# A two-layer decoder trunk on one core: weight sums, a late accumulation and turns put elsewhere in the MLP

## The chip, the cores and the metric

The kernel runs on one core of a Trainium2 chip. A core has TensorE (PE in the profile), VectorE (DVE), ScalarE (ACT), GpSimd (POOL) and SyncE (SP, which here only issues DMAs); GpSimd issues DMAs too, among them those that add to what lies at their destination. The metric is the device time of one execution in microseconds. The kernel before took 1130.81 us, the median of 3 runs (1129.59 to 1131.3).

## What is computed

512 tokens of width 1024 go through two layers. Layer 0 mixes tokens by gated linear attention, layer 1 by stick-breaking attention over shared keys and values. Behind each mixer stand a layer norm, an MLP and another layer norm:

```python
h = layer_norm(DEEPNORM_ALPHA * h + mix, ln_g[layer, 0], ln_b[layer, 0])
h = layer_norm(DEEPNORM_ALPHA * h + sq_relu_mlp(h, mlp_w_up[layer], mlp_w_down[layer]),
               ln_g[layer, 1], ln_b[layer, 1])
...
def sq_relu_mlp(x, w_up, w_down):
    h = jax.nn.relu(x @ w_up)
    return (h * h) @ w_down
```

The MLP's inner width is 4096, all in fp32. The change is in the MLP alone.

## The kernel before

**Products.** A product of fp32 matrices is made from three matmuls: each operand is split into a rounded part `hi` (made by ScalarE: L70 for weights, L98 for activations) and a remainder `lo` (VectorE: L72, L99), and hi·hi, hi·lo and lo·hi are summed. The two MLPs take most of the time: layer 0's from about 207 to 541 us of the span, layer 1's from about 783 to 1111. Between them lie keys, values and attention; the attention's output projection (L1292) ends where layer 1's MLP begins.

**Chunks and steps.** Each MLP runs in four chunks of 1024 of the inner width. A chunk has an `up` product and a `down` product, and each is a 2×2 block product made with seven block products instead of eight, the seven steps of `steps`. So each step needs a sum of activation blocks and a sum of weight blocks. The operands of up are the turned (transposed) tiles T, with the sums in place: step 2 takes `sum3` (L830), step 3 `sum4` (L725 into tmp), step 4 `sum5` (L725 into T), step 5 `sum6` (L842). Those of down are the squared activations s. Matmuls of up are at L899 (48 in a step), of down at L948 (24). After a step VectorE adds the product from PSUM: L915 in up, L167 or L169 in down.

**Weights.** Class `Blocks` holds a product's weights in tiles B of 512 KB, each block in two halves. Block (0,0) and (1,0) are plain; (0,1) and (1,1) are loaded by SP (L741) and then get (0,0) or (0,1) added by an accumulating DMA from GpSimd (L743). Step 3 takes (0,0)+(1,1), which `onto` makes in place just ahead of its splits, and step 6 (1,0)+(0,0). If the block is listed in `by`, the sum is a DMA on GpSimd's queue (L765), otherwise an addition on VectorE (L767). In the last chunk's down of each layer both sums are listed, elsewhere only (1,0) or none. Step 4's weights are a fresh load (`plain`, tiles raw, L64). There are eight B tiles, so the loads for the next product wait until the splits of the current one have read its tiles.

**Start of an MLP.** The four token tiles get their norm one after the other: VectorE makes statistics (L177, L182), GpSimd `ve` and `rs` (L183, L184), VectorE centres the tile (L190), TensorE turns it (L267), ScalarE copies the turned tile (L270). Tiles 2 and 3 are late: their turns are called from within steps 0 and 1 of the first up. The loads of (0,0) and (1,0) of that up are issued by GpSimd (L876) behind a small copy `pin` (L932) which waits for tile 3's `rs`.

**Order.** The program names the order by its writing, and a scheduler of the framework orders each engine's instructions by when it expects them to be ready; instructions passed through `keep` stay in the order in which they are written. Each engine then runs its list strictly in that order. `run_all` makes blocks two steps and operands up to two steps ahead; `between` runs between a step's matmuls and its read.

Of the kernel before, what the change touches and what calls it, by code (L numbers as in the profile page):

```python
# [34 lines left out]
def yoco_kernel(ctx: ExitStack, tc: tile.TileContext, x, gla_w_in, gla_w_a2, gla_b_a, gla_norm_g,  # L35
# [693 lines left out]
    class Blocks:  # L729


        def __init__(self, pool, weights, order, by):
            self.pool, self.w, self.by, self.b = pool, weights, by, {}
            self.load(order)

        def load(self, order, start=lambda **to: nc.sync.dma_start(**to)):
            for k, j, other in order:
                got = []
                for h in range(2):
                    b = self.pool.tile([P, 1024], F32, tag="B", bufs=8, name=nm("B"))  # L740
                    start(out=b.rearrange("p (a b) -> p a b", a=2), in_=self.w(k, h, j))  # L741
                    if other:
                        nc.gpsimd.dma_start(out=b.rearrange("p (a b) -> p a b", a=2), in_=self.w(other[0], h, other[1]),  # L743
                                            accum_op=ALU.add)
                    got.append(b)
                self.b[k, j] = got

# [14 lines left out]
        def onto(self, a, b, h):  # L762
            x, y = self.b[a][h], self.b[b][h]
            if a in self.by:
                keep(nc.gpsimd.dma_start(out=x, in_=y, accum_op=ALU.add))  # L765
            else:
                keep(tt(x, x, y, op=ALU.add))  # L767
            hi, lo = split_tile(x, 2, keep)
            return [(hi[:, i, :], lo[:, i, :]) for i in range(2)]
# [14 lines left out]
    def mlp(l, hT, late, vec, done, ready=None):  # L784
# [26 lines left out]
        def steps(a11, a12, a21, a22, weights, part, read, order, by=(), plain=None, ops=None, after=None):  # L811

            made, t = [], []

# [17 lines left out]

            def sum4():
                minus(t[0], t[0], a11())
                return operand(t[0])

            def sum5(apart=False):
                minus(a12(), a12(), t[0])
                return operand(a12(), apart)

            def sum6(apart=False):
                tt(a11(), a11(), a21(), op=ALU.subtract)  # L842
                return operand(a11(), apart)

            makes = [lambda: operand(a11()), lambda: operand(a12()), sum3, sum4, sum5, sum6, lambda: operand(a22())]
            if ops is not None:
                if not ops:
                    ops.update({0: views([hT.a[0]]), 1: views([hT.a[1]])})
                    kinds = {2: sum3, 3: sum4, 4: lambda: sum5(True), 5: lambda: sum6(True), 6: makes[6]}
                    new = lambda i: (lambda: ops[i]) if i < 2 else (lambda: ops.setdefault(i, kinds[i]()))  # L850
                else:
                    new = lambda i: lambda: ops[i]
                makes = [new(i) for i in range(7)]
# [11 lines left out]
            def step(n):  # L865
# [9 lines left out]
                if after and n == 0:  # L875
                    me.rest = lambda: (after(), made[0].load(AHEAD[:2], lambda **to: keep(nc.gpsimd.dma_start(**to))))  # L876
# [7 lines left out]
        def up(c, also=()):  # L884
# [5 lines left out]
            def part(a, b, banks, opens, closes, n):  # L890
# [3 lines left out]
                for m, (k, f) in enumerate(at):  # L894
                    if c == 0 and late and (n == 0 and m == 13 and len(late) > 1 or n == 1 and m == 4):
                        late.pop(0)()
# [29 lines left out]
            else:  # L926
                plain = [ready[:4], ready[4:]] if ready else [pieces_512(mlp_w_up[l], 512 * k, 4, 0) for k in range(2)]
                last = hs[3].rs

# [4 lines left out]
                made = steps(r[0], r[2], r[1], r[3], w, part, read, AHEAD[2:], ((1, 0),), plain, ops, after)  # L934
# [32 lines left out]
        for c in range(NC):  # L967
# [3 lines left out]
            todo += down(c, q, (range(NT) if l == 0 else (2, 3)) if ends else (), ((0, 0), (1, 0)) if ends else ((1, 0),),  # L971
                         turns[2:] if c == 0 else ())

        def run_all():
            for n, step in enumerate(todo):
# [8 lines left out]
                def between():  # L984
                    if n == 0:
                        step.rest()
                    if n == 1:
                        todo[2].make_operand()
                    if 0 < n <= 5:
# [523 lines left out]
```

## Time and profile before

| what | us |
|---|---|
| median of 3 runs | 1130.81 |
| the profiled execution, its own time | 1129.37 |
| its span, first to last instruction | 1127.6 |
| mean granted TensorE clock | 0.989 of full |

The profile is of one execution, whose own time is 1.77 us above its span and 1.44 us below the median. In a row of a timeline the first number is the start in us of the span, the second the length, then engine, line, operation, tiles and shapes; xN says that N like instructions stand together, and the bracket is the idle time of that engine ahead of the row and what ended it. A row of the table by windows gives, for a stretch, its length, the busy time and count of TensorE, its weight loads, VectorE, ScalarE and GpSimd, the granted clock, the share of time that the DMA engines were busy, and GB/s.

The last rows of the table of groups that bear on the change are these: the two kinds of split, in which VectorE and ScalarE spend the most time.

```profile
L72 DVE TENSOR_TENSOR lo<-B,hi 128x1024 fp32r<-128x1024 f32 x206 | 247.5, 1221 | 84.2 <-ACT hi L70 82.0
L70 ACT ACTIVATE hi<-B 128x1024 fp32r<-128x1024 f32 x206 | 213.5, 1054 | 158.5 <-DVE B L767 65.6
```

### The profile page before, as it was taken

How to read it: one execution, taken by the hardware profiler on the slowest of the kernel's cores; microseconds unless marked ns; L12 is line 12 of the kernel's file. 1: busy time of each engine (PE TensorE's matmuls, PEld its weight loads, DVE VectorE, ACT ScalarE, POOL GpSimd, SP SyncE). 2: the span in 40 equal slices, each digit the busy share in tenths (PEclk: the TensorE clock that was granted, in tenths of full speed). 3: DMA queues.
4: the chain of work that ended last, by engine and by line, in shares of the span. 5: the costliest groups of instructions: out<-in, count | busy, mean ns of one | idle time of the engine just before them, and what ended most of it. 6: DMA issues, size and time to landing. Idle time of an engine off the chain costs nothing. (4 is left out here: it accounts for less than half of the span.)

```text
span 1127.6 us, 16741 instructions
## 1 busy us (share of the span) xinstructions
PE 1091.5 (97%) x6463; PEld 942.9 (84%) x6463; DVE 898.9 (80%) x1083; ACT 669.8 (59%) x963; POOL 182.8 (16%) x217
## 2 busy tenths in 40 slices
PE   9999999989999999999999999997899999999987
PEld 7888888888798898997788787786897988989965
DVE  4488639898988879868898887696989888788667
ACT  4455437676466475564765667765865674655634
POOL 1021210402111111111303001212121011011112
PEclk9999999999999999999999999998999999999989
DMA  7262394779959869687757325456798599597673
GB/s 218 74 182 67 129 256 134 185 215 229 221 155 245 206 154 257 150 222 165 205 126 197 95 87 119 117 135 142 222 245 218 145 222 247 139 244 188 193 180 75
DMA packets 121443, 197.53 MB, mean 175 GB/s; under 512 B 14042, under 2 KB 39002, under 8 KB 121364
## 3 DMA queue, kind: packets, MB, share of 16 engines
q1 hardware_dynamic: 90580, 127.78, 35.4%
q0 software_dynamic: 28320, 63.97, 30.7%
q10 hardware_dynamic: 2464, 4.72, 1.2%
q8 instruction: 51, 0.84, 0.3%
q14 instruction: 28, 0.23, 0.1%
HBM read 176.52 MB, written 3.15 MB: 159 GB/s over the span
## 5 line engine op out<-in xcount | busy, mean ns | idle before, releaser
L72 DVE TENSOR_TENSOR lo<-B,hi 128x1024 fp32r<-128x1024 f32 x206 | 247.5, 1221 | 84.2 <-ACT hi L70 82.0
L70 ACT ACTIVATE hi<-B 128x1024 fp32r<-128x1024 f32 x206 | 213.5, 1054 | 158.5 <-DVE B L767 65.6
L948 PE MATMUL ps<-hi,T 128*128 128x512 f32 x896 | 286.4, 397 | 11.5 <-ACT T L98 8.1
L899 PE MATMUL ps<-T,hi 128*128 128x256 f32 x1280 | 233.0, 284 | 4.4 <-DVE T L99 2.0
L948 PEld LDWEIGHTS ps<-hi,T 128*128 128x128 f32 x896 | 170.7, 191 | 52.6 <-ACT T L98 10.2
L899 PEld LDWEIGHTS ps<-T,hi 128*128 128x128 f32 x1280 | 199.5, 192 | 8.2 <-ACT T L98 2.7
L899 PE MATMUL ps<-T,lo 128*128 128x256 f32 x640 | 179.7, 284 | 3.7 <-DVE lo L72 3.7
L948 PE MATMUL ps<-lo,T 128*128 128x512 f32 x448 | 177.6, 396 | 0.0
L899 PEld LDWEIGHTS ps<-T,lo 128*128 128x128 f32 x640 | 121.9, 192 | 5.0 <-DVE lo L72 4.8
L70 ACT ACTIVATE hi<-raw 128x1024 fp32r<-128x1024 f32 x88 | 91.1, 1057 | 43.5 <-PE ps L94 9.3
L72 DVE TENSOR_TENSOR lo<-raw,hi 128x1024 fp32r<-128x1024 f32 x86 | 103.0, 1217 | 16.5 <-ACT hi L70 16.1
L948 PEld LDWEIGHTS ps<-lo,T 128*128 128x128 f32 x448 | 85.7, 191 | 17.8 <-DVE lo L72 0.7
L899 PE MATMUL ps<-A,hi 128*128 128x256 f32 x512 | 92.5, 283 | 0.0
L98 ACT ACTIVATE T<-s 128x1024 fp32r<-128x1024 f32 (+1 forms) x52 | 51.5, 993 | 53.2 <-DVE s L842 37.0
L93 PE MATMUL ps<-T,hi 128*128 128x512 f32 (+1 forms) x200 | 79.7, 399 | 0.4 <-DVE k L99 0.4
L899 PEld LDWEIGHTS ps<-A,hi 128*128 128x128 f32 x512 | 79.9, 192 | 0.0
L95 PE MATMUL ps<-T,lo 128*128 128x512 f32 (+1 forms) x200 | 76.5, 382 | 0.0
L94 PE MATMUL ps<-T,hi 128*128 128x512 f32 (+1 forms) x200 | 76.4, 382 | 0.0
L743 POOL DMA_DIRECT2D B<-in_mlp_w_down_dram x32 | 38.5, 1202 | 232.0 <-DVE lo L72 103.1
L169 DVE TENSOR_TENSOR h<-h,ps 128x512 f32<-128x512 f32 x108 | 71.4, 680 | 4.2 <-PE ps L948 3.5
L899 PE MATMUL ps<-A,lo 128*128 128x256 f32 x256 | 72.4, 283 | 0.0
L743 POOL DMA_DIRECT2D B<-in_mlp_w_up_dram x32 | 38.8, 1221 | 159.6 <-DMA B<-in_mlp_w_up_dram 45.0
(234 smaller groups left out, 1903.9 us busy)
## 6 DMA issues: line engine op xcount, KB each, us to landing
B<-in_mlp_w_down_dram SPq DMA_DIRECT2D x64, 512.0 KB, 5.3
B<-in_mlp_w_up_dram SPq DMA_DIRECT2D x56, 512.0 KB, 4.8
B<-in_mlp_w_up_dram POOLq DMA_DIRECT2D x40, 512.0 KB, 8.7
B<-in_mlp_w_down_dram POOLq DMA_DIRECT2D x32, 512.0 KB, 9.5
B<-B POOLq DMA_DIRECT2D x28, 512.0 KB, 5.5
raw<-in_mlp_w_up_dram SPq DMA_DIRECT2D x24, 512.0 KB, 5.6
raw<-in_gla_w_in_dram SPq DMA_DIRECT2D x20, 512.0 KB, 3.8
raw<-in_mlp_w_down_dram SPq DMA_DIRECT2D x16, 512.0 KB, 9.8
```

Of the source, the lines that this page charges most:

```text
L70: keep(nc.scalar.activation(hi, raw, AF.Copy))
L72: keep((on or nc.vector).tensor_tensor(lo, raw, hi.bitcast(F32), op=ALU.subtract))
L93: keep(nc.tensor.matmul(ps, lhsT=a[0], rhs=b[0], start=first, stop=False))
L94: keep(nc.tensor.matmul(ps, lhsT=a[0], rhs=b[1], start=False, stop=False))
L95: keep(nc.tensor.matmul(ps, lhsT=a[1], rhs=b[0], start=False, stop=last))
L98: keep(nc.scalar.activation(hi, ps, AF.Copy))
L169: nc.vector.tensor_tensor(h, h, ps, op=op)
L743: nc.gpsimd.dma_start(out=b.rearrange("p (a b) -> p a b", a=2), in_=self.w(other[0], h, other[1]), accum_op=ALU.add)
L899: nc.tensor.matmul(to, lhsT=b[k][x][:, fs], rhs=a(k)[:, y], start=opens and f % 2 == 0 and (k, x, y) == (0, 0, LO), stop=closes and (k, x) ...
L948: nc.tensor.matmul(banks[s], lhsT=a(k)[:, x][:, P * s:P * s + P], rhs=b[k][y], start=opens and (k, x, y) == (0, LO, 0), stop=closes and (k ...
```

## The change

It has four parts.

1. In the last chunk's down of both layers the first weight sum, (0,0)+(1,1), is made by VectorE and no longer by DMAs.
2. In the first up of both layers, `sum4` and the first half of step 3's weight sum are made right behind step 2's operand, ahead of `sum5`; the second half follows later, between the operands. `sum5` and `sum6` there now keep the written order.
3. In layer 1 the accumulation into (1,1) of the first up is issued behind the pin copy, ahead of the loads of (0,0) and (1,0), no longer ahead of and between the norms.
4. The turns of tiles 2 and 3 are called four and three groups of matmuls sooner.

```diff
+        def more(self, got, other, h, keep=lambda ins: ins):
+            keep(nc.gpsimd.dma_start(out=got[h].rearrange("p (a b) -> p a b", a=2), in_=self.w(other[0], h, other[1]),
+                                     accum_op=ALU.add))
...
-        def onto(self, a, b, h):
+        def sum(self, a, b, h):
             x, y = self.b[a][h], self.b[b][h]
+            if (a, h) in self.summed:
+                return
+            self.summed.add((a, h))
             if a in self.by:
                 keep(nc.gpsimd.dma_start(out=x, in_=y, accum_op=ALU.add))
             else:
                 keep(tt(x, x, y, op=ALU.add))
-            hi, lo = split_tile(x, 2, keep)
+
+        def onto(self, a, b, h):
+            self.sum(a, b, h)
+            hi, lo = split_tile(self.b[a][h], 2, keep)
...
+            hold = keep if after else lambda ins: ins
...
+            def minus_a11():
+                minus(t[0], t[0], a11())
+
             def sum4():
-                minus(t[0], t[0], a11())
+                minus_a11()
                 return operand(t[0])
 
             def sum5(apart=False):
-                minus(a12(), a12(), t[0])
+                hold(minus(a12(), a12(), t[0]))
                 return operand(a12(), apart)
 
             def sum6(apart=False):
-                tt(a11(), a11(), a21(), op=ALU.subtract)
+                hold(tt(a11(), a11(), a21(), op=ALU.subtract))
...
-                    kinds = {2: sum3, 3: sum4, 4: lambda: sum5(True), 5: lambda: sum6(True), 6: makes[6]}
+                    kinds = {2: sum3, 3: lambda: operand(t[0]), 4: lambda: sum5(True), 5: lambda: sum6(True), 6: makes[6]}
...
-                    me.rest = lambda: (after(), made[0].load(AHEAD[:2], lambda **to: keep(nc.gpsimd.dma_start(**to))))
+
+                    def rest():
+                        after()
+                        if late_sums:
+                            for h in range(2):
+                                made[0].more(made[0].b[1, 1], (0, 1), h, keep)
+                        made[0].load(AHEAD[:2], lambda **to: keep(nc.gpsimd.dma_start(**to)))
+
+                    me.rest = rest
+                if after and n == 3:
+                    me.sum = lambda: (minus_a11(), made[0].sum((0, 0), (1, 1), 0))
...
-                    if c == 0 and late and (n == 0 and m == 13 and len(late) > 1 or n == 1 and m == 4):
+                    if c == 0 and late and (n == 0 and m == 9 and len(late) > 1 or n == 1 and m == 1):
...
+                first = (AHEAD[2], AHEAD[3] if l == 0 else (1, 1, None))
...
-                made = steps(r[0], r[2], r[1], r[3], w, part, read, AHEAD[2:], ((1, 0),), plain, ops, after)
+                made = steps(r[0], r[2], r[1], r[3], w, part, read, first, ((1, 0),), plain, ops, after,
+                             l == 1)
...
-            todo += down(c, q, (range(NT) if l == 0 else (2, 3)) if ends else (), ((0, 0), (1, 0)) if ends else ((1, 0),),
+            todo += down(c, q, (range(NT) if l == 0 else (2, 3)) if ends else (), ((1, 0),),
                          turns[2:] if c == 0 else ())
...
                         todo[2].make_operand()
+                        todo[3].sum()
```

Line numbers shift: VectorE's weight sum L767 becomes L773, sum3 L830 becomes L840, sum6 L842 becomes L855, GpSimd's accumulation L743 becomes L748 and its loads L876 become L895, the sum by DMA L765 becomes L771, the read L915 becomes L938, pin L932 becomes L956.

How the instructions stand. GpSimd, at the start of layer 1's MLP, before (mv, ve and rs belong to the norms of the tiles 0 to 3, B_7525 and B_7528 are the halves of weight block (1,1), B_7609 to B_7615 those of (0,0) and (1,0)):

```order
L743 DMA B_7525<-in_mlp_w_up_dram 128x2x512
L183 TENSOR_SCALAR ve_7362<-mv_7361 128x1
L184 TENSOR_TENSOR rs_7363<-ve_7362,mhalf 128x1
L743 DMA B_7528<-in_mlp_w_up_dram 128x2x512
L183 TENSOR_SCALAR ve_7383<-mv_7382 128x1
L184 TENSOR_TENSOR rs_7384<-ve_7383,mhalf 128x1
```

The same place in the changed kernel, from the last tile's norm on:

```order
L183 TENSOR_SCALAR ve_7509<-mv_7508 128x1
L184 TENSOR_TENSOR rs_7510<-ve_7509,mhalf 128x1
L956 COPY pin_7605<-rs_7510 128x1
L748 DMA B_7525<-in_mlp_w_up_dram 128x2x512
L748 DMA B_7527<-in_mlp_w_up_dram 128x2x512
L895 DMA B_7609<-in_mlp_w_up_dram 128x2x512
L895 DMA B_7611<-in_mlp_w_up_dram 128x2x512
```

The accumulation into (1,1) has left the place between the norms of tile 0 and tile 1 and now stands ahead of the four loads.

VectorE, in steps 2 and 3 of layer 1's first up, before (tmp and T are the sums of activations, the lo are the remainders for step 3's weights and, for A, step 4's operand):

```order
L725 SCALAR_TENSOR_TENSOR tmp_7689<-tmp_7689,T_7221 128x1024
L725 SCALAR_TENSOR_TENSOR T_7222<-T_7222,tmp_7689 128x4x256
L99 TENSOR_TENSOR T_7695<-tmp_7689,T_7695 128x4x256
L767 TENSOR_TENSOR B_7609<-B_7609,B_7525 128x1024
L842 TENSOR_TENSOR T_7221<-T_7221 128x4x256
L99 TENSOR_TENSOR T_7896<-T_7222,T_7896 128x4x256
L72 TENSOR_TENSOR lo_7701<-B_7609,hi_7699 128x1024
L767 TENSOR_TENSOR B_7611<-B_7611,B_7528 128x1024
L99 TENSOR_TENSOR T_7962<-s_7617,T_7962 128x4x256
L72 TENSOR_TENSOR lo_7706<-B_7611,hi_7704 128x1024
```

and changed:

```order
L725 SCALAR_TENSOR_TENSOR tmp_7689<-tmp_7689,T_7221 128x1024
L773 TENSOR_TENSOR B_7609<-B_7609,B_7525 128x1024
L725 SCALAR_TENSOR_TENSOR T_7222<-T_7222,tmp_7689 128x4x256
L99 TENSOR_TENSOR T_7696<-tmp_7689,T_7696 128x4x256
L72 TENSOR_TENSOR lo_7701<-B_7609,hi_7699 128x1024
L773 TENSOR_TENSOR B_7611<-B_7611,B_7527 128x1024
L99 TENSOR_TENSOR T_7896<-T_7222,T_7896 128x4x256
L99 TENSOR_TENSOR T_7962<-s_7617,T_7962 128x4x256
L72 TENSOR_TENSOR lo_7706<-B_7611,hi_7704 128x1024
```

The first half of the sum is two rows sooner, and L842 is gone from between; as L855 it now stands five rows further on, behind step 4's remainders, and one of two L938 reads stands ahead of the four splits of (1,1) and (1,0).

VectorE, in the last chunk's down of layer 1, before (ps_10344 and ps_10372 are products of steps 0 and 1, B_10165 and B_10167 the halves of (0,0)):

```order
L169 TENSOR_TENSOR h_1639<-h_1639,ps_10344 128x512
L72 TENSOR_TENSOR lo_10361<-B_10165,hi_10359 128x1024
L72 TENSOR_TENSOR lo_10366<-B_10167,hi_10364 128x1024
L99 TENSOR_TENSOR T_10369<-tmp_10325,T_10369 128x4x256
L169 TENSOR_TENSOR h_1638<-h_1638,ps_10372 128x512
L72 TENSOR_TENSOR lo_10404<-raw_10400,hi_10402 128x1024
L169 TENSOR_TENSOR h_1639<-h_1639,ps_10386 128x512
```

and changed:

```order
L169 TENSOR_TENSOR h_1639<-h_1639,ps_10344 128x512
L773 TENSOR_TENSOR B_10165<-B_10165,B_10179 128x1024
L99 TENSOR_TENSOR T_10369<-tmp_10325,T_10369 128x4x256
L169 TENSOR_TENSOR h_1638<-h_1638,ps_10372 128x512
L72 TENSOR_TENSOR lo_10361<-B_10165,hi_10359 128x1024
L773 TENSOR_TENSOR B_10167<-B_10167,B_10182 128x1024
L169 TENSOR_TENSOR h_1639<-h_1639,ps_10386 128x512
L725 SCALAR_TENSOR_TENSOR s_9914<-s_9914,tmp_10325 128x4x256
L72 TENSOR_TENSOR lo_10366<-B_10167,hi_10364 128x1024
```

The two additions stand in VectorE's own list, and the operand and the reads of step 1 go ahead of the second half's split.

More of the change, by code (lines that the diff above doesn't have):

```diff
@@ L732, in __init__ @@
         def __init__(self, pool, weights, order, by):
-            self.pool, self.w, self.by, self.b = pool, weights, by, {}
+            self.pool, self.w, self.by, self.b, self.summed = pool, weights, by, {}, set()
             self.load(order)
@@ L741, in load @@
                     start(out=b.rearrange("p (a b) -> p a b", a=2), in_=self.w(k, h, j))
+                    got.append(b)
                     if other:
-                        nc.gpsimd.dma_start(out=b.rearrange("p (a b) -> p a b", a=2), in_=self.w(other[0], h, other[1]),
-                                            accum_op=ALU.add)
-                    got.append(b)
+                        self.more(got, other, h)
                 self.b[k, j] = got
+        def more(self, got, other, h, keep=lambda ins: ins):
+            keep(nc.gpsimd.dma_start(out=got[h].rearrange("p (a b) -> p a b", a=2), in_=self.w(other[0], h, other[1]),
+                                     accum_op=ALU.add))
         def pieces(self, k, j, keep=lambda ins: ins):
@@ L809, in views, with steps @@
             return lambda k: us[k // n][:, k % n, :]
-        def steps(a11, a12, a21, a22, weights, part, read, order, by=(), plain=None, ops=None, after=None):
+        def steps(a11, a12, a21, a22, weights, part, read, order, by=(), plain=None, ops=None, after=None, late_sums=False):
             made, t = [], []
+            hold = keep if after else lambda ins: ins
             def blocks(k=0, j=0, first=False, sums=None):
```

## The prediction

> **What bounds the kernel now.** The page comes first: which engine is full.
>
> ```profile
> span 1127.6 us, 16741 instructions
> PE 1091.5 (97%) x6463; PEld 942.9 (84%) x6463; DVE 898.9 (80%) x1083; ACT 669.8 (59%) x963; POOL 182.8 (16%) x217
> ```
>
> TensorE is busy for 1091.5 of 1127.6 us. The change takes no matmul away, so it can only win part of the 36.1 us in which TensorE waits, and what these waits cost after them. The second view is TensorE's waits, in us in total, times, longest:
>
> ```profile
> PE ps L948 <- ACT T L98: 8.1, 4, 3.5
> PE ps L267 <- DVE h L190: 8.0, 3, 5.8
> ```
>
> The third is TensorE's timeline, which says where they stand (start, length, what, and in brackets the wait ahead of it):
>
> ```profile
> 243.28 0.39 PE L899 MATMUL ps<-T,lo 128*128 128x256 f32 x1 [0.35 <-DVE lo L72]
> 286.73 0.50 PE L948 MATMUL ps<-hi,T 128*128 128x512 f32 x1 [1.48 <-ACT T L98]
> 541.22 1.06 PE L267 MATMUL ps<-ident,h 128*128 128x128 f32 x8 [1.91 <-DVE h L190]
> 777.37 1.97 PE L267 MATMUL ps<-ident,h 128*128 128x128 f32 x8 [5.85 <-DVE h L190]
> 809.90 0.39 PE L899 MATMUL ps<-T,lo 128*128 128x256 f32 x1 [0.36 <-DVE lo L72]
> 853.35 0.50 PE L948 MATMUL ps<-hi,T 128*128 128x512 f32 x1 [1.48 <-ACT T L98]
> 1089.61 0.79 PE L948 MATMUL ps<-hi,T 128*128 128x512 f32 x1 [3.51 <-ACT T L98]
> 1111.26 0.47 PE L948 MATMUL ps<-hi,T 128*128 128x512 f32 x1 [2.10 <-DVE h L169]
> 1118.19 0.39 PE L948 MATMUL ps<-hi,T 128*128 128x512 f32 x1
> ```
>
> They lie at four places: the start and the end of each layer's MLP. The fourth view, TensorE by windows (busy time and count of each engine, granted clock, DMA share, GB/s), shows that a wait costs more than itself:
>
> ```profile
> 540.00:546.00 6.00, 4.79 (x23) 4.25 (x24) 5.15 (x7) 4.12 (x11) 3.90 (x5) 0.72 0.43 65
> 775.00:780.00 5.00, 2.63 (x11) 2.44 (x12) 3.50 (x5) 1.47 (x5) 1.39 (x3) 0.50 0.69 122
> 1080.00:1085.00 5.00, 5.00 (x23) 4.14 (x23) 0.63 (x1) 1.06 (x1) 0.86 (x1) 1.00 1.06 248
> 1090.00:1095.00 5.00, 4.96 (x12) 3.37 (x12) 5.00 (x6) 1.45 (x2) 0.00 (x0) 0.50 0.24 45
> 853.00:858.00 5.00, 4.59 (x19) 3.47 (x20) 5.00 (x6) 0.30 (x1) 0.00 (x0) 1.00 0.94 319
> ```
>
> At full clock 5 us hold about 22 matmuls of the down product (0.227 us each; a step has 24, so 5.45 us); after the wait of 3.51 they hold 12, at a granted clock of 0.50. I call this a spell. After the wait of 2.10 the step takes from 1111.26 to 1118.42, 7.16 us: 1.7 lost. After 1.48 (853:858) the clock stayed at 1.00. So between 1.48 and 1.91 us a wait begins to cost a spell here (behind 541.22, too, the clock was 0.72). By the same count the spell behind 3.51 cost 3.0, from 1089.61 to 1098.1.
>
> The Trainium skill ("TensorE: Matmul & The Clock Gate", "What's actually happening") says that the clock halves after an idle window of about 3.4 us. The row at 1111.26 speaks against taking that as a limit on one wait: 2.10 us were enough. By the rule, a shorter wait made by the change would cost no spell; the sum would then be that of the clock rival below.
>
> **The change, place by place.** Layers are 0 and 1; in each chunk the up product has steps 0 to 6 and the down product its own 0 to 6.
>
> *Layer 1, start.* What ends the wait of 5.85?
>
> ```profile
> 765.52 0.21 DVE L182 BATCH_NORM_AGGREGATE mv<-bst 128x2 f32<-128x12 f32 x1
> 767.71 1.06 PE L267 MATMUL ps<-ident,h 128*128 128x128 f32 x8 [0.28 <-DVE h L190]
> 769.88 0.19 DVE L182 BATCH_NORM_AGGREGATE mv<-bst 128x2 f32<-128x12 f32 x1
> 774.26 1.26 POOL B L743
> 782.91 0.52 PE L899 MATMUL ps<-T,hi 128*128 128x256 f32 x3
> ```
>
> For tile 0 the transposes start 2.19 us after the statistics (765.52 to 767.71). For tile 1 they should start at 769.88 + 2.19 = 772.1, and start at 777.37: GpSimd stood at an accumulating DMA, which may be issued only when its base has landed (the chain shows 774.26), and the norm's two small operations were queued behind it. The change puts that DMA behind all norms. 5.3 us go, and the spell with them: from 777.37 to 782.91 ran 8 transposes (0.1 each) and 12 matmuls of 0.227, 3.5 us of work in 5.5, so 2.0 more. TensorE is 7.3 us ahead. What is late next?
>
> ```profile
> 798.20 1.23 DVE L725 SCALAR_TENSOR_TENSOR tmp<-tmp,T 128x1024 f32<-128x1024 f32 x1
> 814.44 4.62 DVE L72 TENSOR_TENSOR lo<-B,hi 128x1024 fp32r<-128x1024 f32 x4
> 818.99 1.28 DVE L915 TENSOR_TENSOR s<-s,ps 128x512 f32<-128x512 f32 x2
> 834.47 1.06 ACT L70 ACTIVATE hi<-B 128x1024 fp32r<-128x1024 f32 x1 [1.58 <-DMA B<-in_mlp_w_down_dram]
> 818.00:829.00 11.00, 11.00 (x90) 10.83 (x89) 10.39 (x12) 9.09 (x9) 4.79 (x4) 1.00 1.00 315
> ```
>
> Step 2's operand is made from the turned tiles 2 and 3, a chain through VectorE, GpSimd, TensorE and ScalarE; I let it lose 1.2 of the 7.3, so that the row at 798.20, right behind that operand, comes 6.1 sooner, at 792.1. In step 3 (809.90) the second half's lo has L842, an operation of 1.14 from start to start, no longer ahead of it: about 7.4 sooner. But the first chunk's down product hangs on something else. The four splits at 814.44 free the tiles into which the down weights are loaded. DMA then runs at a share of 1.00 and 315 GB/s, ScalarE waits for it at 834.47, and VectorE works without a pause from there to the operand that TensorE waits for at 853.35. The splits come 6.1 us sooner, less 0.6 for one of the two L915 operations (818.99), now ahead of them, and less 0.9 that I allow for waits for ScalarE's rounding: 4.5 sooner. So TensorE resumes at about 848.8, but arrives 7.4 sooner; its wait grows from 1.48 to about 4.4 and then costs a spell. I price a new spell at 2.0, between 1.7 and 3.0. **Term: −4.5 + 2.0 = −2.5**, bounds −7.3 (all passes) and +3.0 (nothing passes, long spell).
>
> The wait that the change adds: the first sum (L767) of step 3 needs the late accumulation and the loads (L876) behind it.
>
> ```profile
> 788.19 2.98 POOL L876 DMA_DIRECT2D B<-in_mlp_w_up_dram  x4
> B<-in_mlp_w_up_dram POOLq DMA_DIRECT2D x5, 512.0 KB, 6.6
> ```
>
> The loads' issue now begins at 788.19, behind pin. With the norms some 6 us sooner pin comes at 782, two accumulations of 1.26 us of issue (774.26) follow, and the loads begin at 784.6; with 6.6 us from issue to landing the first one lands at 791.9 at the latest (0.75 of issue). The sum stands one operation behind 792.1, at 793.3: a margin of 1.4, and I take no cost. If it is late, the rest of the operand, step 3's operand and the first half's lo are queued behind the sum on VectorE, and step 3 waits for them. On SP the raw loads of up step 4 go ahead of the first two down loads; the bytes are the same, no cost.
>
> *Layer 0, start.* Here nothing is moved on GpSimd. The second half's lo has L842 no longer ahead of it (1.14), and the sooner turns bring step 2's operand some 0.6 forward: step 3 resumes at about 241.6 instead of 243.28, 1.7 sooner. But one L915 more and waits for ScalarE stand ahead of the four splits, which come about 1.0 later, and the same chain (down weights, then VectorE) decides at 286.73. TensorE arrives 1.7 sooner and resumes 0 to 1.0 later, less 0.5 to 0.9 spent in an earlier wait, since matmuls of down's step 0 are pulled ahead of up's step 6: a wait of 2.5 or more, with a spell. **Term: +0.4 + 2.0 = +2.4**, bounds −1.7 and +4.0.
>
> *Layer 0, end.*
>
> ```profile
> 512.36 0.68 DVE L169 TENSOR_TENSOR h<-h,ps 128x512 f32<-128x512 f32 x1
> 516.33 1.23 DVE L72 TENSOR_TENSOR lo<-B,hi 128x1024 fp32r<-128x1024 f32 x1 [2.16 <-ACT hi L70]
> 518.22 1.23 DVE L99 TENSOR_TENSOR T<-tmp,T 128x1024 fp32r<-128x1024 f32 x1 [0.67 <-ACT T L98]
> L767 DVE TENSOR_TENSOR B<-B,B 128x1024 f32<-128x1024 f32 x40 | 48.8, 1219 | 1.0 <-DMA B<-in_mlp_w_up_dram 1.0
> ```
>
> The sum by DMA cost VectorE two pauses, 2.16 and 0.67. Two additions (1.22 us each, 1.14 from start to start) replace them: VectorE ends 0.55 sooner, with L190 ahead of 541.22. TensorE's transposes there now stand seven matmuls later (1.6 us of work put into the wait). 0.55 + 1.6 = 2.1. Within the chunk the second half of the sum gets ready later (six operations of 1.14 and five of 0.60 behind 512.36, so 522.2, where TensorE, seven matmuls into the step, would want it at about 520): a wait of 2.2 and a spell, but beside the VectorE chain that sets the end. **Term: −2.1**, bounds −3.7 (the spell behind 541.22 goes too) and 0.
>
> *Layer 1, end.*
>
> ```profile
> 1077.83 0.68 DVE L169 TENSOR_TENSOR h<-h,ps 128x512 f32<-128x512 f32 x1
> 1084.37 1.23 DVE L72 TENSOR_TENSOR lo<-B,hi 128x1024 fp32r<-128x1024 f32 x1 [5.86 <-ACT hi L70]
> 1087.69 1.22 DVE L72 TENSOR_TENSOR lo<-B,hi 128x1024 fp32r<-128x1024 f32 x1 [2.10 <-ACT hi L70]
> 1110.43 0.68 DVE L169 TENSOR_TENSOR h<-h,ps 128x512 f32<-128x512 f32 x1
> 1077.40 0.86 POOL L765 DMA_DIRECT2D B<-B  x1 [1.61 <-DMA B<-in_mlp_w_down_dram]
> 1083.28 1.06 ACT L70 ACTIVATE hi<-B 128x1024 fp32r<-128x1024 f32 x1 [7.88 <-DMA B<-B]
> ```
>
> The summands are there at 1077.4; the DMA sum needs until 1083.28, VectorE sits idle for 5.86 + 2.10, and TensorE stops for 3.51 behind it. An addition may start at 1078.4. From then to L169 at 1110.43 VectorE had 21.3 us of work (26.1 from 1084.37, less 4.8 idle); with 2.3 for two additions and 1.1 for remaining waits it is there at 1103.0, 7.4 sooner. TensorE without its waits (3.51, 2.10) and spells (3.0, 1.7) would be 10.3 sooner, so VectorE, which works back to back from 1110.43 to the end, is the bound. I take 0.2 more for L169, which now stands ahead of L210. **Term: −7.6**, bounds −10.3 and −2.5.
>
> **Sum:** +2.4 − 2.1 − 2.5 − 7.6 = −9.8. The profiled run took 1129.37 us (span 1127.6): 1119.6. It lies 1.4 below the median of the runs, 1130.81; against that the forecast is **1121.0**.
>
> **Rivals.**
> *Clock:* the new waits cost no spell, or one (853.35 had none after 1.48; 5.85 and 3.51 each had one). −9.8 − 2.0 to −9.8 − 4.0: 1117 to 1119. For: the new waits are estimates. Against: 1.91 and 2.10.
> *DMA keeps layer 1's start:* transfers at a share of 1.00 don't move up, TensorE only waits longer. That term is +2.0: −5.3, 1125.5. For: 1.00 and 1.58. Against: the loads' tiles are freed sooner.
> *VectorE is the bound at the last chunk:* four additions on an engine that has no gap elsewhere; a wait of 2.2 and a spell of 3.0 return, the last term is −2.5: −4.7, 1126.1. Against: 5.86 + 2.10 of idle.
> *Both:* −0.2, no change; nor is there any if the sums' DMAs were hidden anyway, which 7.88 denies.
> *Slower:* the waits aren't removed but moved, and each costs a long spell (3.0). Places: both starts, layer 0's end, two in the last chunk: 15.0 against −9.3, the sum without spells and without layer 1's start (+0.4 − 2.1 − 7.6): +5.7, 1136.5. It decides from four such spells (12.0 − 9.3 = +2.7).
>
> **How the numbers follow.** Forecast 0.56 (own range 1116 to 1124.5), clock 0.12, DMA 0.13, VectorE 0.08, both or nothing 0.06, slower 0.05. The range of 8 in 10, 1112 to 1128, takes in the first four and the terms' bounds. Faster by over 0.2% (2.3 us, about what a measurement can tell from no change) 0.89, within 0.06, slower 0.05.
>
> **What would show it.** Right: no wait over 1 us ahead of tile 1's transposes; VectorE without a pause over 1.2 us in the last down; a wait of 2 to 5 us where 286.73 and 853.35 stand, with a clock under 0.9 behind it. Wrong: the four splits not 4 us sooner; the first sum (L767) waiting for a DMA at layer 1's start; a wait over 2 us in the last chunk.

## The result, and the profile after

The changed kernel takes 1120.67 us, the median of 8 runs (1118.22 to 1123.68), against 1130.2 us of the kernel before (8 runs, 1125.29 to 1132.67). The ratio is 0.9925, with a 95% interval of 0.9904 to 0.9946. The forecast was 1121.0, in a range of 1112 to 1128. The total came out, but of its four terms only one came out by the way that the forecast gave; the errors of the others cancelled, which is luck. The experiments show which.

The page of the changed kernel:

```profile
span 1122.0 us, 16726 instructions
PE 1090.2 (97%) x6463; PEld 940.2 (84%) x6463; DVE 903.0 (80%) x1087; ACT 669.7 (60%) x963; POOL 179.6 (16%) x213
```

VectorE has four instructions more and GpSimd four fewer, as the change says. The profiled execution is the slowest of its eight (1123.68 us), and it reached the first MLP 3.2 us later than the kernel before did (218.79 against 215.57 us of the span), in a stage that the change doesn't touch. So spans are not compared below, but stretches between two marks within one execution.

TensorE's waits in the changed kernel (total us, times, longest):

```profile
PE ps L922 <- DVE T L99: 3.9, 5, 1.5
PE ps L973 <- ACT T L98: 3.9, 2, 1.9
PE ps L973 <- DVE lo L72: 2.4, 3, 1.9
PE ps L267 <- DVE h L190: 0.7, 2, 0.4
```

The turns (L267) now wait 0.7 us for the norm where they waited 8.0, and the down matmuls 3.9 us for ScalarE's operand where it was 8.1. The waits for VectorE's operand in up grew from 2.0 us to 3.9. Where they stand, by TensorE's timeline of the changed kernel:

```profile
282.95 0.73 PE L973 MATMUL ps<-hi,T 128*128 128x512 f32 x2 [1.09 <-DVE T L99]
290.31 0.50 PE L973 MATMUL ps<-hi,T 128*128 128x512 f32 x1 [1.94 <-ACT T L98]
525.95 0.50 PE L973 MATMUL ps<-lo,T 128*128 128x512 f32 x1 [1.87 <-DVE lo L72]
775.67 1.09 PE L267 MATMUL ps<-ident,h 128*128 128x128 f32 x8 [0.41 <-DVE h L190]
802.61 0.39 PE L922 MATMUL ps<-T,hi 128*128 128x256 f32 x1 [1.27 <-ACT hi L70]
1109.72 0.39 PE L973 MATMUL ps<-hi,T 128*128 128x512 f32 x1
1113.85 2.74 PE L1503 MATMUL ps<-h,T 128*128 128x512 f32 x4 [2.02 <-ACT T L1480]
```

The wait of 5.85 is 0.41. In layer 1's last chunk no wait is left that lasts 1 us, and the last matmul starts at 1109.72 instead of 1118.19. But a new wait stands at 802.61, in step 3 of layer 1's first up. VectorE and GpSimd there, in the changed kernel:

```profile
786.23 2.54 POOL L748 DMA_DIRECT2D B<-in_mlp_w_up_dram  x2 [0.31 <-issue]
787.75 3.96 POOL L895 DMA_DIRECT2D B<-in_mlp_w_up_dram  x4
795.54 1.23 DVE L725 SCALAR_TENSOR_TENSOR tmp<-tmp,T 128x1024 f32<-128x1024 f32 x1
800.24 1.23 DVE L773 TENSOR_TENSOR B<-B,B 128x1024 f32<-128x1024 f32 x1 [3.48 <-DMA B<-in_mlp_w_up_dram]
817.65 0.69 DVE L938 TENSOR_TENSOR s<-s,ps 128x512 f32<-128x512 f32 x1 [1.63 <-PE ps L922]
818.26 4.63 DVE L72 TENSOR_TENSOR lo<-B,hi 128x1024 fp32r<-128x1024 f32 x4
```

The first sum (L773) waits 3.48 us for its loads, and the four splits that free the tiles for the down weights stand behind a read of TensorE's product (L938), which waits 1.63. TensorE's clock falls to half behind the wait at 802.61, from 804.3 to 811.2 us; that costs 3.1 us of matmul time. The row by windows in the middle of it, with a clock of 0.50:

```profile
805.00:810.00 5.00, 5.00 (x23) 5.00 (x24) 5.00 (x6) 3.96 (x5) 1.46 (x2) 0.50 0.82 156
```

Four stretches are read in every kernel: **start 0**, from the first up matmul to the last chunk's up step 5 of layer 0; **end 0**, from layer 0's last down to the attention's first matmul; **start 1**, from tile 0's turn (767.71 before, 771.45 after) to layer 1's last down; **end 1**, from there to the end of the span. **Splits** is the time from tile 0's turn to the four splits (814.44 before, 818.26 after). One profiled execution each, in us:

| kernel | start 0 | end 0 | splits | start 1 | end 1 |
|---|---|---|---|---|---|
| before | 274.8 | 106.0 | 46.7 | 301.9 | 58.0 |
| changed | 275.0 | 105.9 | 46.8 | 300.0 | 50.5 |
| undo_a | 274.6 | 109.0 | 46.0 | 300.7 | 57.8 |
| undo_b | 276.6 | 105.4 | 41.7 | 295.8 | 51.2 |
| undo_c | 277.1 | 106.5 | 48.9 | 302.3 | 50.6 |
| undo_d | 275.1 | 104.9 | 46.8 | 300.6 | 51.8 |
| undo_a0 | 276.4 | 104.2 | 47.3 | 302.1 | 51.1 |
| early_sums | 275.0 | 106.4 | 42.4 | 296.6 | 51.1 |
| no_hold | 274.3 | 105.1 | 43.3 | 297.7 | 51.9 |
| early_no_b | 275.4 | 105.1 | 41.4 | 295.0 | 50.3 |
| early_no_hold | 272.7 | 105.7 | 39.5 | 293.3 | 51.5 |
| only_c | 274.3 | 107.6 | 42.1 | 297.4 | 57.1 |
| only_a1 | 274.4 | 104.7 | 45.8 | 299.6 | 51.2 |

Layer 1's last down starts at 1069.59 in the kernel before and at 1071.46 in the changed one. The expectations below quote start 0, both ends and start 1 by marks that lie 0.2 to 1.2 us later (302.1 and 301.2 for start 1, where the marks above give 301.9 and 300.0), so their ranges for these stretches hold with that allowance.

Kernels with the same code in a stretch differ by up to 2.5 us in the starts (start 1: before and only_a1; changed, undo_a, undo_a0) and by up to 4.8 in end 0 (undo_a and undo_a0), mostly by slow-clock spells, so that smaller differences between two rows prove nothing. Splits scatters less: 46.7 and 45.8 for before and only_a1, 46.8, 46.0 and 47.3 for the other three.

### The profile page after: what moved, and what is told of

Read it like the earlier page. It is cut to its first block, busy times and chain, and to the rows that moved or that the text cites. A ratio compares the mean times of both kernels' runs of the same rounds, so it can differ in the third digit from the quotient of the medians.

```text
span 1122.0 us, 16726 instructions
## 1 busy us (share of the span) xinstructions
PE 1090.2 (97%) x6463; PEld 940.2 (84%) x6463; DVE 903.0 (80%) x1087; ACT 669.7 (60%) x963; POOL 179.6 (16%) x213
## 5 line engine op out<-in xcount | busy, mean ns | idle before, releaser
L973 PE MATMUL ps<-hi,T 128*128 128x512 f32 x896 | 281.3, 391 | 7.9 <-ACT T L98 3.9
L922 PE MATMUL ps<-T,hi 128*128 128x256 f32 x1280 | 235.6, 286 | 5.1 <-DVE T L99 3.9
L922 PEld LDWEIGHTS ps<-T,hi 128*128 128x128 f32 x1280 | 201.9, 194 | 8.7 <-DVE T L99 4.9
L973 PEld LDWEIGHTS ps<-hi,T 128*128 128x128 f32 x896 | 167.4, 188 | 47.2 <-DVE T L99 5.6
L973 PE MATMUL ps<-lo,T 128*128 128x512 f32 x448 | 174.9, 391 | 2.4 <-DVE lo L72 2.4
L98 ACT ACTIVATE T<-s 128x1024 fp32r<-128x1024 f32 (+1 forms) x52 | 51.5, 994 | 46.6 <-DVE s L855 39.2
L748 POOL DMA_DIRECT2D B<-in_mlp_w_down_dram x32 | 38.5, 1203 | 244.6 <-DVE lo L72 103.5
L169 DVE TENSOR_TENSOR h<-h,ps 128x512 f32<-128x512 f32 x108 | 71.0, 679 | 1.7 <-PE ps L973 1.7
L99 DVE TENSOR_TENSOR T<-s,T 128x1024 fp32r<-128x1024 f32 (+1 forms) x52 | 59.2, 1138 | 6.7 <-ACT T L98 6.7
```

The costliest lines, as they stand in the source:

```text
L98: keep(nc.scalar.activation(hi, ps, AF.Copy))
L99: keep((on or nc.vector).tensor_tensor(lo, ps, hi.bitcast(F32), op=ALU.subtract))
L169: nc.vector.tensor_tensor(h, h, ps, op=op)
L748: keep(nc.gpsimd.dma_start(out=got[h].rearrange("p (a b) -> p a b", a=2), in_=self.w(other[0], h, other[1]), accum_op=ALU.add))
L922: nc.tensor.matmul(to, lhsT=b[k][x][:, fs], rhs=a(k)[:, y], start=opens and f % 2 == 0 and (k, x, y) == (0, 0, LO), stop=closes and (k, x) ...
L973: nc.tensor.matmul(banks[s], lhsT=a(k)[:, x][:, P * s:P * s + P], rhs=b[k][y], start=opens and (k, x, y) == (0, LO, 0), stop=closes and (k ...
```

## The experiments

### The four parts, each undone alone

**undo_a** makes the last chunk's first sum by DMA again.

```diff
-            todo += down(c, q, (range(NT) if l == 0 else (2, 3)) if ends else (), ((1, 0),),
+            todo += down(c, q, (range(NT) if l == 0 else (2, 3)) if ends else (), ((0, 0), (1, 0)) if ends else ((1, 0),),
```

> The changed kernel with its first part undone: in the last chunk's down of both layers the first weight sum is again made by DMAs. Theory (the two ends differ: in layer 1 the sum by DMA was what the last chunk waited for; in layer 0 whatever the additions win is given back in the values' product, whose start hangs on the norms of tiles 2 and 3): layer 1's waits of 3.5 and 2.1 us and the slow clock behind them return, worth 8.3 us from the start of layer 1's last down to the end of the span; layer 0 from the start of its last down to the start of the attention changes by less than 0.7. Ratio to the kernel before 0.998 to 1.002. Rival (the additions matter at both ends as forecast, 2.1 and 7.6): also 1.5 to 2.5 us more in layer 0, ratio 1.000 to 1.004. Rival (the gain at layer 1's end comes from the other order of VectorE's list, not from the sum): at most 4 us return, ratio 0.994 to 0.997.

Measured: 1129.18 us, ratio to before 0.9988 (0.9965 to 1.0012). End 1 went from 50.5 to 57.8 us, and the wait came back:

```profile
1091.17 0.79 PE L973 MATMUL ps<-hi,T 128*128 128x512 f32 x1 [3.54 <-ACT T L98]
```

So layer 1's last chunk carries nearly all of the gain. End 0 took 109.0, which neither theory had; undo_a0 tests it.

**undo_b** drops the sooner half sums and the written order.

```diff
-            hold = keep if after else lambda ins: ins
+            hold = lambda ins: ins
...
-                    kinds = {2: sum3, 3: lambda: operand(t[0]), 4: lambda: sum5(True), 5: lambda: sum6(True), 6: makes[6]}
+                    kinds = {2: sum3, 3: sum4, 4: lambda: sum5(True), 5: lambda: sum6(True), 6: makes[6]}
...
-                if after and n == 3:
-                    me.sum = lambda: (minus_a11(), made[0].sum((0, 0), (1, 1), 0))
...
-                        todo[3].sum()
```

> The changed kernel with its second part undone: sum4 and the first half of the weight sum are again made in their old places, and the two other operand sums aren't held in order. Theory (the first chunk's down product decides, so the sooner half sums win nothing in layer 0; in layer 1 the first sum waits for its loads anyway): from the start of the MLP to its second chunk both layers change by less than 1 us; in layer 1 VectorE's wait for the DMA shrinks from 3.5 to 1.5 or less, since the sum stands two operations later. Ratio to the changed kernel 0.999 to 1.001 (to the kernel before 0.991 to 0.995). Rival (the half sums carry what the starts gained): each start loses 1.5 to 2 us, ratio to before 0.995 to 0.998.

Measured: 1118.63 us, ratio to before 0.9912 (0.9885 to 0.9939). Both theories fell in layer 1: start 1 is 4.2 us shorter without this part (295.8), though the first sum is made at the same distance from tile 0's turn as in the changed kernel (29.0 and 28.8 us; the turn is at 769.12 us of the span in this execution), so the loads are as late as there:

```profile
798.13 1.23 DVE L773 TENSOR_TENSOR B<-B,B 128x1024 f32<-128x1024 f32 x1 [1.29 <-DMA B<-in_mlp_w_up_dram]
810.84 4.63 DVE L72 TENSOR_TENSOR lo<-B,hi 128x1024 fp32r<-128x1024 f32 x4
```

From the first sum to the splits it takes 12.7 us here, 18.0 in the changed kernel (800.24 to 818.26). So the part's order costs layer 1 about 5 us in the same chain in which the third part was to win 4.5. In layer 0 start 0 took 1.6 us more without it, which is within the scatter.

**undo_c** puts the accumulations back between the norms.

```diff
-                first = (AHEAD[2], AHEAD[3] if l == 0 else (1, 1, None))
+                first = AHEAD[2:]
...
-                             l == 1)
+                             False)
```

> The changed kernel with its third part undone: in layer 1 the accumulation into (1,1) stands ahead of and between the norms again. Theory (moving it removed a wait of 5.4 us and 2 us of slow clock, and made the loads behind it late, so that the first sum waited 3.5 us for a DMA, with a slow spell): the wait of about 5.8 ahead of tile 1's turn returns, VectorE's wait for the loads at the first sum is under 0.5, and from the projection to layer 1's second chunk it takes 0 to 2 us more than the changed kernel. Ratio to before 0.992 to 0.996. Rival (the loads are late because the sum was moved ahead by the second part, not because of the accumulations): the sum still waits 2 us or more, and the stretch takes 4 to 7 us more, ratio 0.996 to 0.999.

Measured: 1125.47 us, ratio to before 0.9956 (0.9932 to 0.998), start 1 302.3, which is 2.3 us longer than in the changed kernel. The wait is back, and the first sum waits no more for a DMA:

```profile
781.76 1.97 PE L267 MATMUL ps<-ident,h 128*128 128x128 f32 x8 [5.78 <-DVE h L190]
804.40 1.22 DVE L773 TENSOR_TENSOR B<-B,B 128x1024 f32<-128x1024 f32 x1
```

So the late loads came with the moved accumulations, as the theory had it; with both the wait and the order of part two, the stretch is no better than before.

**undo_d** calls the turns at 13 and 4 again.

```diff
-                    if c == 0 and late and (n == 0 and m == 9 and len(late) > 1 or n == 1 and m == 1):
+                    if c == 0 and late and (n == 0 and m == 13 and len(late) > 1 or n == 1 and m == 4):
```

> The changed kernel with its fourth part undone: the turns of tiles 2 and 3 are called where they were. Theory (these turns hang on the norms, not on where TensorE's list has them, and what follows is decided by the loads): both layers change by less than 0.8 us from the MLP's start to its second chunk. Ratio to before 0.991 to 0.995. Rival (they set step 2's operand, which comes 1.2 us later without them): each start loses 1 to 1.5 us, ratio 0.994 to 0.997.

Measured: 1121.63 us, ratio 0.9928 (0.9902 to 0.9954). Start 0 and start 1 change by 0.1 and 0.6 us: the turns' place is worth nothing that can be told here.

### The two costs of layer 1's start, taken away

**early_sums** issues the accumulations behind tile 1's norm, ahead of tile 2's.

```diff
-                        after()
                         if late_sums:
+                            keep(nc.gpsimd.tensor_copy(out=small(1, "pin"), in_=hs[1].rs))
                             for h in range(2):
                                 made[0].more(made[0].b[1, 1], (0, 1), h, keep)
+                        after()
...
-                    nc.gpsimd.tensor_copy(out=small(1, "pin"), in_=last)
+                    keep(nc.gpsimd.tensor_copy(out=small(1, "pin"), in_=last))
```

> The changed kernel with layer 1's two accumulations issued behind tile 1's norm (a second small copy that waits for its rs) and ahead of tile 2's, so that the four loads are the only ones behind the last norm. The stretch read is from tile 0's turn to the start of layer 1's last down: 302.1 us in the kernel before, 301.2 in the changed one, 296.3 with the second part undone. Theory (the first sum waits because two accumulations of 512 KB go ahead of its loads in the same burst): VectorE's wait for a DMA at the first sum falls from 3.5 to under 1 us, no slow spell behind it, and the stretch takes 296.5 to 299. Rival (the order on VectorE, with a read of TensorE's product ahead of the four splits, costs the 5 us, not the DMA): the wait goes, but the stretch stays at 300 to 301.5. Rival (the burst is limited by its bytes): the wait stays over 2 us.

Measured: 1117.85 us, ratio to before 0.9895 (0.9867 to 0.9923). The first sum waits for nothing, the splits come 4.4 us sooner than in the changed kernel (42.4 against 46.8), and start 1 is 3.4 shorter:

```profile
794.21 1.22 DVE L773 TENSOR_TENSOR B<-B,B 128x1024 f32<-128x1024 f32 x1
810.20 0.69 DVE L939 TENSOR_TENSOR s<-s,ps 128x512 f32<-128x512 f32 x1 [0.23 <-PE ps L923]
810.80 4.62 DVE L72 TENSOR_TENSOR lo<-B,hi 128x1024 fp32r<-128x1024 f32 x4
```

The theory holds: the two accumulations in the same burst made the loads late. From issue to landing the four loads took these times, in the kernel before, in the changed one and in early_sums (the least is that of the first load):

```profile
DMA to landing us min/median/max: 4.0/7.0/8.9
DMA to landing us min/median/max: 12.4/14.2/15.4
DMA to landing us min/median/max: 4.4/6.3/8.9
```

In the changed kernel the two accumulations and the four loads are issued in one go on GpSimd's queue, and no run tells whether the loads were late because they stood behind the accumulations there or because the DMA engines had more to move at once. The read ahead of the splits (here L939) waits 0.23 us where it waited 1.63: most of that wait, too, came from the late loads.

**no_hold** keeps the sooner half sums, but lets the scheduler place sum5 and sum6.

```diff
-            hold = keep if after else lambda ins: ins
+            hold = lambda ins: ins
```

> The changed kernel without the written order for sum5 and sum6 (the sooner half sums stay). VectorE's list then has both reads (L938) behind the four splits and sum6 between the halves, as before. Theory (a read that waits for TensorE's step 3 ahead of the splits holds back the loads of the down product): the stretch from tile 0's turn to layer 1's last down takes 296 to 298.5, though the first sum still waits 3 us or more for its loads; in layer 0 the stretch from the MLP's start to its last up takes 0 to 1 us less than the changed kernel's 275.4. Rival (the late loads decide): 300 to 301.5 in layer 1.

Measured: 1116.85 us, ratio 0.988 (0.9847 to 0.9913). The loads are as late as ever, yet the splits come 3.5 us sooner (43.3 against 46.8) and start 1 takes 297.7, which is 2.3 under the lowest of the three kernels with the changed kernel's code here (300.0, 300.7 and 302.1):

```profile
796.12 1.23 DVE L773 TENSOR_TENSOR B<-B,B 128x1024 f32<-128x1024 f32 x1 [4.17 <-DMA B<-in_mlp_w_up_dram]
809.89 4.62 DVE L72 TENSOR_TENSOR lo<-B,hi 128x1024 fp32r<-128x1024 f32 x4
```

Its list on VectorE differs from the changed kernel's in what stands ahead of the splits: sum6 comes between the half sums, both reads (L938) and step 6's operand come behind the splits. From the first sum to the splits it takes 13.8 us here and 18.0 in the changed kernel; 4.0 of the 4.2 between them are the waits of 1.63 and 0.70 (the latter for ScalarE), the read itself (0.6) and step 6's operand (1.1). So of the second part it is mostly the written order that costs. The sooner sums alone cost 1.6 us where the loads are late (splits at 43.3, in undo_b at 41.7) and win 1.9 where they are not (early_no_hold 39.5, early_no_b 41.4).

**early_no_b** is early_sums with undo_b's edit.

> The changed kernel with the accumulations behind tile 1's norm and the second part undone. Theory (two separate costs: the late loads, and the order on VectorE): the stretch from tile 0's turn to layer 1's last down takes 293 to 296, under the 296.3 of the second part undone alone; layer 0's start is that of undo_b. Ratio to the kernel before 0.986 to 0.991. Rival (one cost: with either cause gone the stretch is at its floor): 296 to 297.5, ratio 0.990 to 0.993.

Measured: 1116.83 us, ratio 0.9886 (0.9857 to 0.9915), start 1 295.0. That lies in the theory's stretch, but only 0.9 under undo_b, within the scatter; it doesn't tell the theory from its rival.

**early_no_hold** takes both edits, early_sums and no_hold.

> The changed kernel with both costs of layer 1's start taken away: the accumulations behind tile 1's norm, and no written order for sum5 and sum6; the sooner half sums stay. Theory (late loads and the read ahead of the splits are two causes that meet at the same chain, whose floor is the loads of the down weights): the stretch from tile 0's turn to layer 1's last down takes 294.5 to 296.5 us (early_sums 297.5, no_hold 298.2, early_no_b 295.9), layer 0's from the MLP's start to its last up 274.5 to 275.5; ratio to the kernel before 0.984 to 0.989. Rival (the causes are independent and add up, 3.6 and 3.0 us): 294 or less, ratio under 0.985.

Measured: 1113.05 us, ratio to before 0.9856 (0.9827 to 0.9884), the fastest kernel of the study. Its VectorE list runs from the first sum to the splits without a wait (the pauses of 3.48 and 1.63 are gone):

```profile
790.95 1.22 DVE L773 TENSOR_TENSOR B<-B,B 128x1024 f32<-128x1024 f32 x1
804.71 4.63 DVE L72 TENSOR_TENSOR lo<-B,hi 128x1024 fp32r<-128x1024 f32 x4
```

Start 1 took 293.3 us. The rival is the nearer one, though the ratio is not under its 0.985: the two gains add up (3.4 + 2.3 off 300.0 would be 294.3), and no floor of the loads shows. Of the 6.7 us, 2.9 are TensorE's waits in the stretch, which fell from 8.3 us to 5.4, and 3.1 are the spell of the changed kernel, which this execution does not have. A spell follows at this place in all seven kernels that issue the accumulations behind all norms, between 798 and 805 us, and in early_sums and early_no_hold there is none (early_no_b has one at 794.6).

### Where parts stand alone

**undo_a0** makes the sum by DMA in layer 0's last chunk only.

```diff
-            todo += down(c, q, (range(NT) if l == 0 else (2, 3)) if ends else (), ((1, 0),),
+            todo += down(c, q, (range(NT) if l == 0 else (2, 3)) if ends else (), ((0, 0), (1, 0)) if ends and l == 0 else ((1, 0),),
```

> The changed kernel with the first part undone in layer 0 alone. The stretch read is from the start of layer 0's last down to the attention's first matmul: 105.5 us before, 105.4 changed, 104.9, 106.1 and 104.0 in the three others with the additions, 108.8 with the sum by DMA in both layers. Theory (the additions are worth 3 us in layer 0 within the changed order; that the changed kernel shows nothing against before is because another part takes as much): 107.5 to 109.5. Rival (the 108.8 was scatter, three slow spells in one execution): 104.5 to 106.5. Layer 1's end as in the changed kernel, 49.4 us from its last down to the end of the span, within 1.5.

Measured: 1122.43 us, ratio 0.9931 (0.9903 to 0.9958). End 0 took 104.2, less than any kernel with the additions; the theory fell, and the 109.0 of undo_a was scatter: two spells in this stretch cost it 4.7 us of matmul time, and undo_a0 had none there. The eight kernels with the additions took 104.9 to 106.5, the five without 104.2 to 109.0. In layer 0 the additions win nothing that can be told.

**only_c** is the kernel before with the accumulations behind the norms (the edits of undo_a, undo_b and undo_d together).

> The kernel before with the third part alone (the accumulations behind all norms). Theory (the third part is worth its forecast 4.5 us as long as the second part's order doesn't hold back the splits): the stretch from tile 0's turn to layer 1's last down takes 296 to 298.5 against 302.1 before; the rest as before, ratio 0.994 to 0.998. Rival (the late loads take the gain by themselves): 300 to 301.5, ratio 0.998 to 1.000.

Measured: 1126.58 us, ratio to before 0.9977 (0.9955 to 0.9998). Start 1 is 297.4 against 301.9: 4.4 us off, as the term of the forecast had it before its spell, although the first sum still waits 1.7 us for its loads. Part of it may be scatter, since only_a1, which has the code of the kernel before in this stretch, took 299.6; the splits come 4.6 and 3.7 us sooner than in these two.

**only_a1** is the kernel before with the additions in layer 1's last chunk (undo_a0, undo_b, undo_c and undo_d together).

> The kernel before with the first part alone, and that in layer 1's last chunk alone. Theory (the term of layer 1's end stands by itself, bounded by VectorE): from layer 1's last down to the end of the span it takes 49.4 to 51.5 us against 57.8 before, the rest as before; ratio 0.992 to 0.996. Rival (the gain needs the other parts, which let the loads of the last chunk come sooner): 53 to 56 us, ratio 0.996 to 0.999.

Measured: 1121.18 us, ratio to before 0.9925 (0.9894 to 0.9955). End 1 is 51.2 against 58.0. This one part, at one place, gives as much as the whole change.

## Why the prediction came out, step by step

**Layer 1, end: forecast −7.6, measured −7.5; right.** In the thirteen executions end 1 took 50.3 to 51.9 with the additions and 57.1 to 58.0 without, means 51.1 and 57.6, so −6.5 on average. VectorE sets the end, as forecast; its rows in the changed kernel, last chunk:

```profile
1080.59 1.22 DVE L773 TENSOR_TENSOR B<-B,B 128x1024 f32<-128x1024 f32 x1
1083.46 1.22 DVE L72 TENSOR_TENSOR lo<-B,hi 128x1024 fp32r<-128x1024 f32 x1
1102.36 1.88 DVE L169 TENSOR_TENSOR h<-h,ps 128x512 f32<-128x512 f32 x3
1105.30 0.15 DVE L210 TENSOR_SCALAR T<-T 128x1 f32<-128x1 f32 x1 [0.29 <-ACT T L209]
```

From the first addition to the third L169 of the row at 1102.36 VectorE has no pause that a bracket would show: the idle 5.86 + 2.10 are gone. TensorE runs through the whole last down without a wait. Its last matmul came 10.3 us sooner within the stretch (from 1118.19 to 1109.72, and the last down had started 1.9 later), which is the forecast's sum of the waits and spells, and the tail behind it gave 2.9 back, since VectorE ends it.

**Layer 1, start: forecast −4.5 + 2.0 = −2.5, measured −1.9, which is within the scatter of nothing and near the forecast by luck.** Its first half was right: the wait went from 5.85 to 0.41 us, step 2 began 7.1 us sooner after tile 0's turn (22.1 against 29.2), and the chain from the four splits is as the forecast drew it: in all thirteen kernels start 1 ends 253.2 to 255.3 us behind the splits, whether these come at 39 or at 49. The step that failed is "the splits come 4.5 sooner"; they came 0.1 later. Two of its figures were wrong. The landing: "6.6 us from issue to landing", a margin of 1.4; the first load took 12.4, and the median of the six was 13.0, as this row of the changed kernel's DMA issues from 770 to 810 us shows:

```profile
B<-in_mlp_w_up_dram POOLq DMA_DIRECT2D x6, 512.0 KB, 13.0
```

The two accumulations, the four loads and SP's own ran as one burst; the window from 795 to 800 us of the changed kernel has the DMA engines busy for a share of 1.05, at 352 GB/s:

```profile
795.00:800.00 5.00, 4.44 (x37) 4.44 (x38) 1.73 (x2) 3.53 (x4) 0.00 (x0) 1.00 1.05 352
```

And the read put ahead of the splits, priced at its own 0.6 us: it brought a wait for TensorE's step 3 with it (1.63 at 817.65), which was itself late by the first wait, and step 6's operand (1.1 us) was put ahead of the splits too. early_sums and no_hold take one each away and win 3.4 and 2.3; both together 6.7, so that the term could have been −8.6. That the late loads might stall the sum was named, with its queue, and taken at no cost. The spell that the forecast took away at the start (2.0 us) came back behind the new waits (3.1 us lost from 804.3 on), and the one that it put behind the wait at the first down did not come: that wait was 1.93 us, where about 4.4 were forecast, and passed at full clock. Of the three signs that the forecast named for being wrong, two came: the splits were not sooner, and the first sum waited for a DMA.

**Layer 0, start: forecast +2.4, measured +0.2; mis-sized.** TensorE's wait grew from 1.48 to 1.94 (290.31) and not to 2.5 or more, since a wait of 1.09 for VectorE (282.95) stands 7 us ahead of it; and the spell priced at 2.0 did not come. It came in undo_c and undo_a0, whose code is the same in this stretch, and they took 277.1 and 276.4 against 274.6 to 275.0 of the changed kernel, undo_a and early_sums: the spell's price was right, but it doesn't come every time.

**Layer 0, end: forecast −2.1, measured −0.1; wrong.** Its first part held: the norm was 0.55 us sooner (the turn moved from 541.22 to 544.13, while the last down started 3.45 later). The second part, "1.6 us of work put into the wait", counted matmuls that TensorE does while it waits as a gain, and did not ask what is late behind the turns. It is ScalarE: from the first copy of the turned tile it works without a pause to the rounding that the next product needs. ScalarE in the changed kernel, and TensorE behind it:

```profile
544.80 1.85 ACT L270 ACTIVATE s<-ps,bcol,gcol 128x128 f32<-128x128 f32 x5 [6.01 <-PE ps L267]
551.85 1.15 ACT L70 ACTIVATE hi<-raw 128x1024 fp32r<-128x1024 f32 x1
553.05 1.02 PE L1076 MATMUL ps<-hi,T 128*128 128x512 f32 x2 [1.04 <-ACT hi L70]
```

In the kernel before the same two ScalarE rows stand at 541.88 and 548.95, so both are 0.5 us sooner within the stretch, like the norm. TensorE reached the values' product 3.8 us sooner and waited there. This is read from the trace; no run tests it, and the scatter of end 0 (4.8 us) is wider than the term.

**The rivals.** "DMA keeps layer 1's start" had the right place, by another way: not the down weights' loads, but the up weights' own. Its term of +2.0 did not come. "VectorE is the bound at the last chunk" was right as to the bound and wrong as to the price, since no wait came back. The total came out because errors cancelled: the two starts made −1.7 us where −0.1 was forecast, the two ends −7.6 where −9.7 was.

## What to carry to other kernels

A transfer moved out of a queue's way comes back as a rival for the queue and the bandwidth at its new place: before it is costed at nothing, count the bytes that run in its new window beside it, and look for a window where the DMA engines idle (here the stretch behind tile 1's norm, which early_sums uses). A write order imposed to bring one operation forward also fixes what comes ahead of the operations behind it; a read of another engine's result there costs that engine's lateness, not its own duration. And work that fills a wait is a gain only if what follows does not hang on the end of that wait through another engine.

## What the runs showed of the hardware

A slow-clock spell lasts about 3.4 us or twice that, whatever the wait ahead of it: of the 39 spells that begin behind 190 us and end before the span does, in the thirteen profiles, 30 last 3.4 to 3.5 us and nine 6.9. Here is the kernel before, behind its wait of 2.10 us, by windows of 1 us:

```profile
1112.00:1113.00 1.00, 1.00 (x5) 0.72 (x3) 1.00 (x1) 0.60 (x2) 0.96 (x1) 0.69 0.07 16
1113.00:1114.00 1.00, 1.00 (x4) 0.81 (x3) 0.97 (x4) 0.46 (x1) 1.00 (x2) 0.50 0.00 0
1114.00:1115.00 1.00, 1.00 (x4) 0.81 (x3) 1.00 (x2) 0.69 (x1) 0.05 (x2) 0.50 0.00 0
1115.00:1116.00 1.00, 1.00 (x4) 0.77 (x4) 0.86 (x2) 0.25 (x1) 0.88 (x1) 0.60 0.00 0
```

The granted clock is down by 0.31, 0.50, 0.50 and 0.40, together 1.71 us of matmul time lost, which at half clock is 3.4 us. Whether a wait brings one is a matter of more than its length. A spell came behind a wait as short as 1.59 us (526.38 us of the kernel before, which the forecast's list of waits leaves out). Over the thirteen profiles a drop followed, within 4 us, 23 of 42 waits of 1.8 to 2.25 us, and each of the five of 3.4 us or more; but of four waits of 3.18 to 3.23 us ahead of the same turn only two. In undo_a0 one passed at full clock; its row of TensorE's timeline:

```profile
542.84 1.06 PE L267 MATMUL ps<-ident,h 128*128 128x128 f32 x8 [3.22 <-DVE h L190]
```

and the window behind it, with a clock of 1.00:

```profile
543.00:544.00 1.00, 1.00 (x10) 0.96 (x10) 1.00 (x3) 0.50 (x2) 1.00 (x2) 1.00 0.00 0
```

while undo_a's of 3.22 us at 542.53 was followed by six windows at 0.50. The Trainium skill ("TensorE: Matmul & The Clock Gate", "What's actually happening") describes a free-running window of about 3.4 us; the spell's length agrees with it, and so does that the same wait counts in one execution and not in the next. That only a wait of a whole window halves the clock does not agree: 23 shorter ones did. So in this kernel a wait of about 2 us is priced at 2 + 0.5 × 1.7 us, and a single execution can't tell changes under some 2.5 us at one place.
